# Values of two strided groups as seven half-sized products, behind the third head's projections

## The chip, the cores and the metric

The kernel runs on one core of one Trainium2 chip. The metric is the device time of one execution in microseconds (us). The kernel before takes 1063.59 us (median of 3 runs, 1063.26 to 1063.8).

## The reference

One layer of a hybrid decoder for 512 tokens of width 1024, all in f32. One input projection gives queries, keys and values of three causal token mixers and three gates; the mixers' outputs are gated, added, projected and normed; a squared-ReLU MLP follows. The change is in the values of the third mixer, the dilated attention. Cut to what matters:

```python
DIL_PAIRS = ((128, 1), (512, 4), (2048, 16))   # window, dilation of three head groups, four heads of 128 each
x @ W_in -> da_q da_k da_v (4 heads)  sb_q sb_k sb_v (8 heads)  dl_q dl_k dl_v (3 groups x 4 heads)  gates (3 x 1024)

def dilated_group(q, k, v, bias_table, window, dilation):
    # query t reads keys and values t, t-d, ..., t-window: to_strided puts them in order of t mod d
    logits = einsum(qs, kb) * dh ** -0.5 ; + bias ; causal window
    lse = logsumexp(logits) ; prob = exp(logits - lse)
    o = einsum(prob, vb)
    return o, lse
# the outputs of the three groups of a head slot are combined by softmax over their lse

m = sum_i sigmoid(gate_i) * (branch_i @ W_i)
x = LayerNorm(alpha * x + m @ W_out)
x = LayerNorm(alpha * x + relu(x @ W_up)**2 @ W_down + sigmoid(x @ W_g) * (p @ W_p))
```

The values of the two strided groups (dilation 4 and 16) are two products of x (512 tokens x 1024) with weights of 1024 x 512.

## The kernel before

**Precision.** A product of f32 matrices is made of three matmuls. Each operand is split into a part rounded to the matmul's format and the rest (`wh` and `wl` of a weight, `xh` and `xl` of x), and high x high, high x low and low x high are added up in PSUM. So one output tile of 128 x 512 with a contraction of 1024 takes 8 x 3 = 24 matmuls.

**Weights.** A block of 512 KB (128 x 1024) goes from DRAM into a ring of raw blocks (`raw`, RAW = 7) by a transfer on SP's queue, issued in a fixed order as soon as the block seven places earlier has been used (`fill`). ScalarE casts it to `wh` (L212), VectorE subtracts to `wl` (L214); these two are in a ring of RING = 7 blocks each. `pump` splits blocks ahead up to the ring's size. Other tiles of 128 x 512 (queries, keys, values, forms of x) come from a pool of NSLOT = 42 slots.

**Items.** `main_order` writes out the order of the projection. A "T" item is one tile of queries or keys for 128 columns of weights (L87 to L89, 24 matmuls, one weight block). A "V" item is one tile of values for 128 tokens (L340 to L342, 24 matmuls); four of them share four weight blocks. The loop at the end of `trunk` issues the items one after another and calls `step()` once or twice for each, which advances what stands in `pending`: generators of the attention heads, tables and forms. So the matmuls of a head are put between those of the items, and each engine executes its instructions in the order thus written. A head of the dilated mixer starts when its six T items are done: its logits (L1496 for group 0, L1512 for groups 1 and 2), the bias and the row maxima (VectorE, L1499 and L1520), exponentials (ScalarE, L1505 and L1527), the folding of the maxima and denominators of the three groups (L1530 to L1559), the scaling of the weights (VectorE, L1561 and L1565), their transposes (PE, L1577 and L1586) with evacuations (L96, L98), and the products with the values (L1598, L1603). Only these last ones need the values.

**Strided values.** The values of group 0 are used in the order of the tokens. Those of groups 1 and 2 are needed by residue of the token mod 4: each V item is copied into half a block of the raw ring (a block without a load, `src` None), and four transfers of 64 KB on SP's queue put its rows (`t[c::4]`) into four slots, `by[g][c]`. LAND = 6 steps later they may be used (`by_residue`).

**Order of the values.** In before the three groups' values stand behind the three pairs of T items of the second head (h = 1), one group behind each pair.

**Sums and forms.** Some later products (gates and MLP) are done by Strassen-Winograd's scheme: seven products of half the size instead of eight. It needs sums of weight blocks, which `sum_steps` makes in DRAM ahead of time by copying and accumulating transfers on POOL's queue (L825, L823); the main loop spreads them by a credit of RATES per item, from item 16 on. It also needs sums of parts of x (`mixer_forms`): eight transfers of 256 KB into slots `xr` on POOL's queue, VectorE's differences (L432 to L450), and a split of each of them (cast on ScalarE, L237, and difference on VectorE, L238). The tables of the differential heads are made at item DA_TABS = 41.

Of the kernel before, what the change touches and what calls it, by code (L numbers as in the profile page):

```python
# [10 lines left out]
F32 = mybir.dt.float32  # L11
# [3 lines left out]
OP = mybir.AluOpType  # L15
# [3 lines left out]
P = 128  # L19
# [16 lines left out]
def main_order():  # L36


    o = [("T", "sb_q", 0), ("T", "sb_k", 0), ("T", "sb_q", 1), ("T", "sb_k", 1), ("V", "sb_v", 0)]
    for j in (2, 3):  # L40
        o += [("T", "sb_q", j), ("T", "sb_k", j)]
    for h in range(4):
        for g in range(3):
            o += [("T", "dl_q", 4 * g + h), ("T", "dl_k", 4 * g + h)]
            if h == 1:
                o += [("V", "dl_v", g)]
    for h in range(4):
        o += [("T", "da_q", h), ("T", "da_k", h)]
        if h == 1:
            o += [("V", "da_v", 0)]  # L50
    for j in range(8):
        o += [("T", "gate", 8 + j)]
    return o


def trunk(tc, a, out):
    nc = tc.nc
    es = ExitStack()
    with es:
# [14 lines left out]
        def slot(name, dt=F32):  # L74
            return big.tile([P, 512], dt, name=nm(name), tag="s", bufs=NSLOT)

# [16 lines left out]
        def cp(o, i):  # L93
            flip[0] ^= 1
            if flip[0]:
                nc.scalar.copy(o, i)  # L96
            else:
                nc.vector.tensor_copy(o, i)  # L98
# [220 lines left out]

        by = {}  # L320
        LAND = 6

        def by_residue(g):
            for _ in range(LAND):
                yield
            for c in range(4):
                V["dl_v", g, c] = by[g][c]

        def v_items(nv, name, g):
            blocks = [{"src": None, "w": 1024, "uses": 2, "own": False} for _ in range(2)]  # L330
            if name == "dl_v" and g > 0:
                items[-2]["blocks"] = blocks
            cs = [chunk(a["wv"][nv, c].rearrange("p k n -> p (k n)"), 1024) for c in range(4)]
            for tt in range(4):
                def mm(ps, tt=tt):
                    for k in range(8):
                        c = cs[k // 2]
                        s = slice((k % 2) * 512, (k % 2) * 512 + 512)
                        x1, x2 = xh[k][:, tt * P:tt * P + P], xl[k][:, tt * P:tt * P + P]
                        nc.tensor.matmul(ps, x1, c["h"][:, s], start=k == 0, stop=False)  # L340
                        nc.tensor.matmul(ps, x1, c["l"][:, s], start=False, stop=False)  # L341
                        nc.tensor.matmul(ps, x2, c["h"][:, s], start=False, stop=k == 7)  # L342
                        if k == 3:
                            yield

                def ev(ps, tt=tt):
                    if name == "sb_v":
                        v = [slot(name, F32R).rearrange("p (h two d) -> p h two d", two=2, d=64) for _ in range(2)]
                        pv = ps.rearrange("p (h d) -> p h d", d=64)
                        for i in range(2):  # L350
                            hs = slice(4 * i, 4 * i + 4)
                            nc.scalar.copy(v[i][:, :, 0, :], pv[:, hs, :])
                            nc.vector.tensor_sub(v[i][:, :, 1, :], pv[:, hs, :], v[i][:, :, 0, :].bitcast(F32))
                        V[name, g, tt] = v
                    elif g == 0:
                        t = slot(name)
                        cp(t, ps)
                        V[name, g, tt] = t
                    else:

                        b = blocks[tt // 2]
                        t = b["raw"][:, (tt % 2) * 512:(tt % 2) * 512 + 512]
                        cp(t, ps)
                        if tt == 0:
                            by[g] = [slot(name) for _ in range(4)]
                        for c in range(4):
                            nc.sync.dma_start(by[g][c][32 * tt:32 * tt + 32, :], t[c::4, :])
                        b["uses"] -= 1
                        if tt == 3:
                            pending.append(by_residue(g))  # L370
                item(cs if tt == 3 else [], mm, ev, need=cs)

        nt, nv = 2, 0
# [2 lines left out]
        for kind, name, j in order[2:]:  # L376
            if kind == "T":
                if name == "gate":
                    continue
                t_item(nt, name, j)  # L380
                nt += 1
            else:
                v_items(nv, name, j)
                nv += 1


# [11 lines left out]
                nc.scalar.activation(t, t, AF.Sigmoid, scale=sign)  # L398
            sg[i, j] = t

        HB = slice(0, 256)
        HC = slice(256, 512)
# [4 lines left out]

        def mixer_forms():

            r = {}  # L410
            for h in range(2):
                for th in range(2):
                    for kp in range(2):
                        t = slot("xr")
                        i = nc.gpsimd.dma_start(t.rearrange("p (k t) -> p k t", k=2),
                                                xt[:, 4 * h + 2 * kp:4 * h + 2 * kp + 2, 256 * th:256 * th + 256])
                        tc.add_manual_dep(getattr(i, "ins", i), lows[-1].name, mybir.DependencyInfo(
                            mybir.DependencyClass.Sync, mybir.DependencyReason.DATA), reason="not ahead of time")
                        r[h, th, kp] = t
            r11, r12, r21, r22 = [[r[h, th, kp] for kp in range(2)] for h in range(2) for th in range(2)]  # L420

            def form(p, r):
                fs = [split(r[kp], f"u{p}") for kp in range(2)]
                xf[p] = [[fs[k // 2][i].rearrange("p (k t) -> p k t", k=2)[:, k % 2, :] for i in range(2)]
                         for k in range(4)]
# [7 lines left out]
            form(7, r22)  # L433
# [6 lines left out]
            form(6, r11)  # L440
            yield
            assert not plain_left[0]
            for kp in range(2):
                t = r12[kp].rearrange("p (k t) -> p k t", k=2)
                h, lo = [x[:, 2 * kp:2 * kp + 2, HC] for x in (xhT, xlT)]
                nc.scalar.copy(h, t)
                nc.vector.tensor_sub(lo, t, h.bitcast(F32))
            yield
            for kp in range(2):
                nc.vector.scalar_tensor_tensor(r21[kp], r11[kp], -1.0, r21[kp], op0=OP.mult, op1=OP.subtract)  # L450
            form(4, r21)
            yield

        def branch_item(i, j):
# [339 lines left out]
        dsum = [[dram.tile([P, 1024], F32, name=f"dsum{m}_{i}") for i in range(4)] for m in range(ND - 1)]  # L794

        def sum_steps():
            def up_steps(sums, w):
                w = [w[i].rearrange("p k n -> p (k n)") for i in range(4)]
# [31 lines left out]
            todo = deque(up_steps(gsum[m], a["wg"][m]) for m in range(2))  # L830
# [1015 lines left out]
```

## Time and profile before

| | |
|---|---|
| median of 3 runs | 1063.59 us |
| profiled execution, its own time | 1063.83 us |
| its span | 1062.1 us |
| granted TensorE clock | 0.998 |
| PE (matmul) busy | 1050.6 us |
| DVE (VectorE) busy | 750.0 us |
| ACT (ScalarE) busy | 558.5 us |
| POOL (GpSimd) busy | 130.1 us |
| moved by DMA | 208.21 MB, mean 196 GB/s |

The profile is of one execution. Its span runs from the first instruction to the last; the execution's own time has 1.7 us more around it. In a row of the timeline stand start, duration, engine, line, operation and output <- inputs. In a row of a group stand the line, engine, operation, output <- inputs, shapes, count, then busy time in us and mean duration in ns, then the engine's idle time just before these instructions with what released it. Engines: PE matmul, PEld weight load, DVE VectorE, ACT ScalarE, POOL GpSimd, SP the queue of the weight loads.

### The profile page before, as it was taken

To read this page: it belongs to the slowest core of one execution; us is meant where nothing else is said; L and a number is where in the kernel's file an instruction comes from. 1 tells how busy PE (TensorE), PEld (TensorE's weight loads), DVE (VectorE), ACT (ScalarE), POOL (GpSimd) and SP (SyncE) were. 2 spreads that over 40 slices of the span, in tenths; PEclk is the share of its full clock that TensorE was granted. 3 is DMA by queue.
4 is the path that set the end of the run, shared out by engine and by line. 5 is a ranking of instruction groups with operands and counts; after the bars stand their busy time and mean duration, and the time that the engine had idled before them with its cause. 6 is when DMAs were issued, how large, how long until landed. Compare 5 with 4: busy or idle time off the path is not lost.

```text
span 1062.1 us, 15599 instructions
## 1 busy us (share of the span) xinstructions
PE 1050.6 (99%) x5826; PEld 904.5 (85%) x5826; DVE 750.0 (71%) x1345; ACT 558.5 (53%) x975; POOL 130.1 (12%) x200
## 2 busy tenths in 40 slices
PE   9999999999999999999999999999999999999996
PEld 6888788888888888888999988888999989989885
DVE  6888667548253757768777773888777877877965
ACT  6666545525232546547545452675766665665741
POOL 0000402021121102230111030101110010000000
PEclk9999999999999999999999999999999999999999
DMA  8433656395896819773766583149989688867502
GB/s 314 134 130 99 210 149 168 140 297 135 315 245 193 235 38 316 153 244 98 200 180 202 175 290 137 67 138 268 269 282 276 235 239 255 259 229 244 189 14 79
DMA packets 60987, 208.21 MB, mean 196 GB/s; under 512 B 7944, under 2 KB 8856, under 8 KB 60912
## 3 DMA queue, kind: packets, MB, share of 16 engines
q1 hardware_dynamic: 37728, 125.76, 34.0%
q0 software_dynamic: 22608, 80.55, 29.4%
q8 instruction: 45, 0.74, 0.3%
q10 hardware_dynamic: 576, 0.92, 0.2%
q14 instruction: 30, 0.25, 0.1%
HBM read 202.97 MB, written 73.42 MB: 260 GB/s over the span
## 4 chain that ended last, share of the span: by engine, by line
PE 88%; DVE 7%; issue 2%; ACT 2%; DMA 0%; POOL 0%; SPq 0%; DVEq 0%; POOLq 0%
PE mm L87 13%; PE mm L89 13%; PE mm L88 13%; PE at L87 4%; PE at L983 4%; PE at L984 4%; PE at L985 4%; PE at L88 4%; PE at L89 4%; PE mm L340 3%; PE mm L342 3%; PE mm L341 3%; DVE wl L214 2%; PE at L131 1%; PE at L312 1%
## 5 line engine op out<-in xcount | busy, mean ns | idle before, releaser
L212 ACT CAST wh<-raw 128x1024 fp32r<-128x1024 f32 (+1 forms) x243 | 250.5, 1034 | 253.7 <-PE mm L88 154.5
L214 DVE TENSOR_TENSOR wl<-raw,wh 128x1024 fp32r<-128x1024 f32 (+1 forms) x243 | 291.5, 1205 | 109.8 <-ACT wh L212 106.4
L87 PE MATMUL mm<-xhT,wh 128*128 128x512 f32 x368 | 146.8, 399 | 0.0
L89 PE MATMUL mm<-xhT,wl 128*128 128x512 f32 x368 | 144.4, 392 | 0.0
L88 PE MATMUL mm<-xlT,wh 128*128 128x512 f32 x368 | 144.1, 392 | 0.0
L89 PEld LDWEIGHTS mm<-xhT,wl 128*128 128x128 f32 x368 | 69.1, 188 | 15.0 <-DVE wl L214 0.3
L87 PEld LDWEIGHTS mm<-xhT,wh 128*128 128x128 f32 x368 | 69.2, 188 | 13.6 <-issue 0.4
L88 PEld LDWEIGHTS mm<-xlT,wh 128*128 128x128 f32 x368 | 69.2, 188 | 13.1
L983 PE MATMUL at<-wh,hh 128*128 128x512 f32 x188 | 73.7, 392 | 0.0
L984 PE MATMUL at<-wl,hh 128*128 128x512 f32 x188 | 73.7, 392 | 0.0
L87 PE MATMUL mm<-x1hT,wh 128*128 128x256 f32 x256 | 73.6, 288 | 0.0
L985 PE MATMUL at<-wh,hl 128*128 128x512 f32 x188 | 73.1, 389 | 0.0
L88 PE MATMUL mm<-x1lT,wh 128*128 128x256 f32 x256 | 72.3, 283 | 0.0
L89 PE MATMUL mm<-x1hT,wl 128*128 128x256 f32 x256 | 71.8, 283 | 0.0
L340 PE MATMUL mm<-wh,xhT 128*128 128x512 f32 x160 | 63.4, 396 | 0.0
L342 PE MATMUL mm<-wh,xlT 128*128 128x512 f32 x160 | 62.5, 391 | 0.0
L341 PE MATMUL mm<-wl,xhT 128*128 128x512 f32 x160 | 62.4, 390 | 0.0
L823 POOL DMA_DIRECT2D usum<-in_wu_dram x32 | 28.0, 874 | 232.8 <-DVE wl L214 199.4
L87 PEld LDWEIGHTS mm<-x1hT,wh 128*128 128x128 f32 x256 | 48.8, 190 | 4.7 <-ACT up L917 2.7
L88 PEld LDWEIGHTS mm<-x1lT,wh 128*128 128x128 f32 x256 | 48.8, 191 | 1.5
L89 PEld LDWEIGHTS mm<-x1hT,wl 128*128 128x128 f32 x256 | 48.6, 191 | 0.0
L823 POOL DMA_DIRECT2D dsum<-in_wd_dram x28 | 26.1, 930 | 139.1 <-DVE wl L214 134.8
(437 smaller groups left out, 2538.4 us busy)
## 6 DMA issues: line engine op xcount, KB each, us to landing
usum<-in_wu_dram POOLq DMA_DIRECT2D x48, 512.0 KB, 8.8
raw<-in_wt_dram SPq DMA_DIRECT2D x46, 512.0 KB, 5.7
dsum<-in_wd_dram POOLq DMA_DIRECT2D x42, 512.0 KB, 9.1
raw<-usum SPq DMA_DIRECT2D x32, 512.0 KB, 6.4
raw<-dsum SPq DMA_DIRECT2D x28, 512.0 KB, 4.7
raw<-in_wd_dram SPq DMA_DIRECT2D x25, 512.0 KB, 4.4
raw<-in_wu_dram SPq DMA_DIRECT2D x24, 512.0 KB, 6.1
raw<-in_wv_dram SPq DMA_DIRECT2D x20, 512.0 KB, 5.0
```

The lines of the kernel that those rows point to most:

```text
L87: nc.tensor.matmul(ps, wh, xh, start=start, stop=False, skip_group_check=True)
L88: nc.tensor.matmul(ps, wh, xl, start=False, stop=False, skip_group_check=True)
L89: nc.tensor.matmul(ps, wl, xh, start=False, stop=stop, skip_group_check=True)
L212: i = nc.scalar.copy(h, raw)
L214: i = nc.vector.tensor_sub(lo, raw, h.bitcast(F32))
L340: nc.tensor.matmul(ps, x1, c["h"][:, s], start=k == 0, stop=False)
L341: nc.tensor.matmul(ps, x1, c["l"][:, s], start=False, stop=False)
L342: nc.tensor.matmul(ps, x2, c["h"][:, s], start=False, stop=k == 7)
L823: i = nc.gpsimd.dma_start(o, i, accum_op=OP.add, max_dma_last_dim=4096)
L983: nc.tensor.matmul(ps, h[:, q], c["h"][:, s], start=go, stop=False, skip_group_check=True)
L984: nc.tensor.matmul(ps, h[:, q], c["l"][:, s], start=False, stop=False, skip_group_check=True)
L985: nc.tensor.matmul(ps, lo[:, q], c["h"][:, s], start=False, stop=end, skip_group_check=True)
```

## The change

The values of group 0 stay behind the first pair of T items of the second head. Those of groups 1 and 2 move behind all six T items of the third head and become one block product: x is cut into halves of the tokens and of the contraction, the weights into the two groups and the halves of the contraction, and seven products (p) of half the contraction and half the tokens, in the order 2, 1, 7, 6, 4, 5, 3, take the place of eight. Each is two items (row halves) of 12 matmuls of 128x512, of size 0.5, without a step in their middle: 14 items with 168 matmuls for 8 with 192. They use 14 weight blocks for 8; eight of these (products 7, 6, 5, 3) come from `vsum`, weight sums in DRAM, whose 16 transfers are put first in the queue of sums. `value_forms` loads eight `xr` tiles and makes and splits the sums of x. Evacuations add up the products: 12 operations of VectorE and 6 copies of ScalarE for 8 copies. The results of products 1, 4, 5 and 3 go into raw blocks and from there by 32 transfers of 64 KB, as before. Products 5 and 3 share a PSUM bank each: 3 adds onto 5's sum once that has been read.

Besides, RING goes from 7 to 6 and NSLOT from 42 to 46; the sums start at item 12 at a rate of 1.8 (16 and 1.6 before); DA_TABS goes from 41 to 47; `mixer_forms` shares `load_xr` and `form` with the new forms.

```diff
@@ main_order
-            if h == 1:
+            if h == 1 and g == 0:
                 o += [("V", "dl_v", g)]
+        if h == 2:
+            o += [("V", "dl_v", 1), ("V", "dl_v", 2)]
@@
-        NSLOT = 42
+        NSLOT = 46
-        RING, RAW = 7, 7
+        RING, RAW = 6, 7
@@
+        vf = {p: [(xh[k][:, c], xl[k][:, c]) for k in range(ks, ks + 4)] for p, ks, c in ((1, 0, HB), (2, 4, HB), (3, 4, HC))}
+        vsum = [[dram.tile([P, 1024], F32, name=f"vsum{m}_{i}") for i in range(4)] for m in range(2)]
...
+        def form(to, p, r):
+            fs = [split(r[kp], f"u{p}") for kp in range(2)]
+            to[p] = ...
+        def value_forms():
+            r11, r12, r21, r22 = load_xr()
+            for _ in range(WAIT):
+                yield
+            with tc.issue_after(st["low"]):
+                for kp in range(2):
+                    nc.vector.tensor_sub(r22[kp], r22[kp], r12[kp])
+            form(vf, 7, r22)
+            yield
+            yield
+            for kp in range(2):
+                with tc.issue_after(st["low"]):
+                    nc.vector.tensor_sub(r12[kp], r11[kp], r12[kp])
+                nc.vector.scalar_tensor_tensor(r11[kp], r22[kp], -1.0, r11[kp], op0=OP.mult, op1=OP.subtract)
+            form(vf, 6, r11)
+            yield
+            yield
+            for kp in range(2):
+                nc.vector.scalar_tensor_tensor(r21[kp], r11[kp], -1.0, r21[kp], op0=OP.mult, op1=OP.subtract)
+            form(vf, 4, r21)
+            yield
+            yield
+            form(vf, 5, r12)
+            yield
+        WAIT = 8
+        def value_pair(nv):
+            v_from[:] = len(items) - 5, len(items)
...
+            for p in (2, 1, 7, 6, 4, 5, 3):
+                for r in range(2):
+                    if not r:
+                        blk = {1: 0, 2: 2, 4: 6}.get(p)
+                        cs[p] = [chunk(vsum[kp][{5: 0, 6: 1, 7: 2, 3: 3}[p]] if blk is None else w[blk + kp], 1024)
+                                 for kp in range(2)]
...
+                    def bank(p=p, r=r):
+                        if p == 5:
+                            x[r] = at_bank()
+                        return x[r] if p in (5, 3) else at_bank() if r else mm_bank()
+                    def mm(ps, p=p, r=r):
+                        for k in range(4):
...
+                            nc.tensor.matmul(ps, h[:, q], c["h"][:, n], start=go, stop=False, skip_group_check=True)
+                            nc.tensor.matmul(ps, h[:, q], c["l"][:, n], start=False, stop=False, skip_group_check=True)
+                            nc.tensor.matmul(ps, lo[:, q], c["h"][:, n], start=False, stop=end, skip_group_check=True)
+                    def ev(ps, p=p, r=r):
+                        if p in (2, 7):
+                            s[p, r] = slot("vs")
+                            nc.scalar.copy(s[p, r], ps)
+                        elif p == 1:
+                            s[1, r] = slot("vs")
+                            nc.vector.tensor_add(put(1, r), s.pop((2, r)), ps)
+                            nc.scalar.copy(s[1, r], ps)
+                            send(1, r, 1, 0)
+                        elif p == 6:
+                            nc.vector.tensor_add(s[1, r], s[1, r], ps)
+                            nc.vector.tensor_add(s[7, r], s[7, r], s[1, r])
+                        elif p == 3:
+                            nc.vector.tensor_add(put(3, r), s[1, r], ps)
+                            send(3, r, 1, 1)
+                        else:
+                            nc.vector.scalar_tensor_tensor(put(p, r), s[7, r], -1.0, ps, op0=OP.mult,
+                                                           op1=OP.subtract)
+                            send(p, r, 2, int(p == 5))
+                    item(cs[p] if r else [], mm, ev, need=cs[p], bank=bank, size=0.5)
@@ sum_steps
+            todo = deque(up_steps(vsum[m], [w[2 + i // 2, i % 2 * 2 + m] for i in range(4)], True) for m in range(2))
+            todo.extend(up_steps(gsum[m], a["wg"][m]) for m in range(2))
@@ main loop
-        DA_TABS = 41
+        DA_TABS = 47
-        RATES = 1.6, 1.0
+        RATES = 1.8, 1.0
+            if n == v_from[0]:
+                pending.append(value_forms())
-            if 16 <= n < wout_at - 6:
+            if 12 <= n < wout_at - 6:
```

More of the change, by code (lines that the diff above doesn't have):

```diff
@@ new lines, in load_xr @@
+        def load_xr():
+            r = {}
+            for h in range(2):
+                for th in range(2):
+                    for kp in range(2):
+                        t = slot("xr")
+                        i = nc.gpsimd.dma_start(t.rearrange("p (k t) -> p k t", k=2),
+                                                xt[:, 4 * h + 2 * kp:4 * h + 2 * kp + 2, 256 * th:256 * th + 256])
+                        tc.add_manual_dep(getattr(i, "ins", i), lows[-1].name, mybir.DependencyInfo(
+                            mybir.DependencyClass.Sync, mybir.DependencyReason.DATA), reason="not ahead of time")
+                        r[h, th, kp] = t
+            return [[r[h, th, kp] for kp in range(2)] for h in range(2) for th in range(2)]
@@ new lines, in trunk, with put, send @@
+        WAIT = 8
+        def value_pair(nv):
+            v_from[:] = len(items) - 5, len(items)
+            cs, s, x = {}, {}, {}
+            outs = {p: {"src": None, "w": 1024, "uses": 2, "own": False} for p in (1, 4, 5, 3)}
+            w = [a["wv"][nv + n, c].rearrange("p k n -> p (k n)") for n in range(2) for c in range(4)]
+            def put(p, r):
+                return outs[p]["raw"][:, r * 512:r * 512 + 512]
+            def send(p, r, g, th):
+                tt = 2 * th + r
+                if g not in by:
+                    by[g] = [slot("dl_v") for _ in range(4)]
+                for c in range(4):
+                    nc.sync.dma_start(by[g][c][32 * tt:32 * tt + 32, :], put(p, r)[c::4, :])
+                outs[p]["uses"] -= 1
+            for p in (2, 1, 7, 6, 4, 5, 3):
[4 more added lines that the diff above has]
+                                 for kp in range(2)]
+                        if p in outs:
+                            items[-3]["blocks"] = [outs[p]]
+                    def bank(p=p, r=r):
[3 more added lines that the diff above has]
+                    def mm(ps, p=p, r=r):
+                        q = slice(r * P, r * P + P)
+                        for k in range(4):
+                            c = cs[p][k // 2]
+                            n = slice(k % 2 * 512, k % 2 * 512 + 512)
+                            h, lo = vf[p][k]
+                            go, end = k == 0 and p != 3, k == 3 and p != 5
+                            nc.tensor.matmul(ps, h[:, q], c["h"][:, n], start=go, stop=False, skip_group_check=True)
[20 more added lines that the diff above has]
+                            send(p, r, 2, int(p == 5))
+                        if (p, r) == (3, 1):
+                            pending.append(by_residue())
+                    item(cs[p] if r else [], mm, ev, need=cs[p], bank=bank, size=0.5)
@@ L358, in ev @@
                         V[name, g, tt] = t
[L359 to L370, printed above, removed]
                 item(cs if tt == 3 else [], mm, ev, need=cs)
@@ L382, in trunk @@
             else:
-                v_items(nv, name, j)
+                if name != "dl_v" or j == 0:
+                    v_items(nv, name, j)
+                elif j == 1:
+                    value_pair(nv)
                 nv += 1
@@ L408, in mixer_forms @@
         def mixer_forms():
[L410 to L425, printed above, removed]
+            r11, r12, r21, r22 = load_xr()
             for _ in range(8):
@@ L796, in sum_steps, with up_steps @@
         def sum_steps():
-            def up_steps(sums, w):
-                w = [w[i].rearrange("p k n -> p (k n)") for i in range(4)]
+            def up_steps(sums, w, flat=False):
+                w = [w[i] if flat else w[i].rearrange("p k n -> p (k n)") for i in range(4)]
                 a1, a2, a3, a4 = sums
@@ L828, in issue @@
                     mybir.DependencyClass.Sync, mybir.DependencyReason.DATA), reason="spread over the main stream")
-            todo = deque(up_steps(gsum[m], a["wg"][m]) for m in range(2))
+            w = a["wv"].rearrange("g c p k n -> g c p (k n)")
+            todo = deque(up_steps(vsum[m], [w[2 + i // 2, i % 2 * 2 + m] for i in range(4)], True) for m in range(2))
+            todo.extend(up_steps(gsum[m], a["wg"][m]) for m in range(2))
             for m in range(ND):
```

26 lines of the change are left out of this document (14 added, 12 removed).

## The prediction

> **What bounds the kernel now.** I read the page first (busy shares, slices, chain), then PE's waits, then PE's timeline for the price of a matmul, then windows of 20 us around the place to which the work moves, then VectorE by group and in order.
>
> ```profile
> PE 1050.6 (99%) x5826; PEld 904.5 (85%) x5826; DVE 750.0 (71%) x1345; ACT 558.5 (53%) x975; POOL 130.1 (12%) x200
> PE 88%; DVE 7%; issue 2%; ACT 2%; DMA 0%; POOL 0%; SPq 0%; DVEq 0%; POOLq 0%
> PE at L1153 <- DVE zero L1150: 1.3, 1, 1.3
> PE at L1444 <- DVE lg L1439: 0.6, 2, 0.4
> ```
>
> TensorE is busy for 1050.6 of 1062.1 us, the chain that ended last is 88% PE, and of the waits that the view names for PE the longest is 1.3 us, at the start. So a matmul taken away is time taken away, as long as nothing else makes PE wait. VectorE is second, with 71% on average; an average hides stretches, so it is read by stretch below. The profiled execution took 1063.83 us, 1.7 us more than its span and 0.24 us above the median of 1063.59. I make the sum against 1063.83 and take 0.24 off at the end. About 0.2%, 2.1 us, is what a measurement of this kernel tells from no change: below 1061.5 is faster, above 1065.7 slower.
>
> **1. The matmuls removed.** The two strided groups' values are 8 items of 24 matmuls of 128x512, 192 in all. Seven products of two row halves with 12 matmuls each are 168. 24 go. A duration would price them wrongly:
>
> ```profile
> 84.46 0.39 PE L87 MATMUL mm<-xhT,wh 128*128 128x512 f32 x1
> 84.69 0.39 PE L88 MATMUL mm<-xlT,wh 128*128 128x512 f32 x1
> ...
> 89.90 0.39 PE L87 MATMUL mm<-xhT,wh 128*128 128x512 f32 x1
> ```
>
> Each lasts 0.39 us, but from 84.46 to 89.90 there are 24 starts, so one costs 5.44 / 24 = 0.2267 us. 24 of them are **5.4 us**, not the 9.4 that 24 x 0.39 would give. This term has no cover: it is on the path.
>
> **2. VectorE in the stretch that receives the values.** The values now stand behind the third head's six projections, and the first two dilated heads' softmaxes, which need the values only at their end, run beside them. In before the same two heads and the third group's values fall here:
>
> ```profile
> 240.00:260.00 20.00, 20.00 (x119) 17.51 (x118) 15.49 (x83) 13.34 (x41) 2.19 (x3) 1.00 0.34 99
> 260.00:280.00 20.00, 20.00 (x98) 16.77 (x97) 9.85 (x21) 5.36 (x8) 4.44 (x8) 1.00 1.03 362
> 280.00:300.00 20.00, 20.00 (x110) 17.36 (x109) 3.83 (x4) 4.65 (x6) 4.67 (x7) 1.00 0.80 225
> L214 DVE TENSOR_TENSOR wl<-raw,wh 128x1024 fp32r<-128x1024 f32 x9 | 11.0, 1221 | 8.8 <-ACT wh L212 8.8
> L291 DVE COPY dl_k<-mm 128x512 f32<-128x512 f32 x3 | 2.1, 692 | 17.2 <-PE mm L89 17.2
> L98 DVE COPY raw<-mm 128x512 f32<-128x512 f32 x2 | 1.4, 688 | 6.9 <-PE mm L342 6.9
> ```
>
> The window rows give, after the range, its length and then busy time of PE, PEld, DVE, ACT and POOL, granted clock, DMA share, GB/s; the three lower rows are VectorE's groups from 238 to 300 us. VectorE is busy for 15.49 + 9.85 + 3.83 = 29.2 us of 60. Less 11.0 of weight splits, 2.1 and 1.4 of copies, two heads are 14.7 us by durations. A head has some 35 small operations, and those start later than they last:
>
> ```profile
> 261.95 0.20 DVE L1558 RECIPROCAL mxx<-mxx 128x8 f32<-128x8 f32 x1
> 262.19 0.17 DVE L1559 TENSOR_TENSOR mxx<-mxx,ex 128x8 f32<-128x8 f32 x1
> 262.39 1.08 DVE L1561 TENSOR_SCALAR L<-L,mxx 128x128 f32<-128x128 f32 x4
> ```
>
> 0.24 us from start to start against 0.20. With 70 x 0.04 = 2.8 more, two heads take about 17.6 us. The large operations go the other way. The gate products of before, which use the same kind of forms, show it:
>
> ```profile
> 480.00:500.00 20.00, 20.00 (x117) 17.57 (x116) 18.82 (x32) 15.84 (x29) 1.53 (x3) 1.00 0.25 82
> 491.05 0.69 DVE L447 TENSOR_TENSOR xlT<-xr,xhT 128x512 fp32r<-128x512 f32 x1
> 491.78 0.69 DVE L238 TENSOR_TENSOR u6l<-xr,u6h 128x512 fp32r<-128x512 f32 x1
> 492.39 0.68 DVE L447 TENSOR_TENSOR xlT<-xr,xhT 128x512 fp32r<-128x512 f32 x1
> 492.99 0.69 DVE L238 TENSOR_TENSOR u6l<-xr,u6h 128x512 fp32r<-128x512 f32 x1
> 493.60 0.68 DVE L468 TENSOR_TENSOR graw<-graw,mm 128x512 f32<-128x512 f32 x1
> 494.19 0.69 DVE L450 SCALAR_TENSOR_TENSOR xr<-xr,xr 128x512 f32<-128x512 f32 x1
> 494.80 1.22 DVE L214 TENSOR_TENSOR wl<-raw,wh 128x1024 fp32r<-128x1024 f32 x1
> 495.93 0.42 DVE L523 TENSOR_TENSOR graw<-at,up 128x256 f32<-128x256 f32 x1
> ```
>
> An operation of 0.69 us is followed after 0.60 (491.78, 492.39, 492.99, 493.60, 494.19), a weight split of 1.22 after 1.13 (494.80, 495.93). In the built order of the changed program these stand on VectorE between the first head's first logits and the last evacuation of the seven products: 16 weight splits (14 of the products, two of neighbours), 14 form operations, 12 evacuations and the two heads: 16 x 1.13 + 26 x 0.60 + 17.6 = **51.3 us**. PE's work there: 14 half items, 168 x 0.2267 = 38.1, one projection 5.4 (24 matmuls), and the two heads' logits and transposes:
>
> ```profile
> L1512 PE MATMUL at<-dl_k,dl_q 128*128 128x128 f32 x32 | 4.0, 277 | 0.0
> L1496 PE MATMUL at<-dl_k,dl_q 128*128 128x256 f32 x12 | 2.9, 380 | 0.0
> L1586 PE MATMUL at<-ident,L 128*128 128x128 f32 x16 | 2.1, 272 | 0.0
> L1577 PE MATMUL at<-ident,L 128*128 128x128 f32 x14 | 2.0, 272 | 0.0
> ```
>
> 11.0 us in these groups of PE between 238 and 270 us, which overlap like the matmuls above; I take 8. Together **51.5 us**. The two engines are equal. That has two consequences. VectorE's waits inside the heads are no longer free:
>
> ```profile
> L1530 DVE TENSOR_TENSOR r<-st,exf 128x32 f32<-128x32 f32 x2 | 0.4, 188 | 2.0 <-ACT L L1505 2.0
> L1533 DVE TENSOR_TENSOR r<-st,exf 128x32 f32<-128x32 f32 x2 | 0.4, 192 | 1.0 <-ACT L L1527 0.9
> L1543 DVE TENSOR_TENSOR sel<-at,pick 128x64 f32<-128x64 f32 x2 | 0.4, 221 | 0.9 <-PE at L1539 0.9
> ```
>
> 3.9 us in these three groups, for two heads. Unfilled, they make 51.3 + 3.9 - 51.5 = 3.7 us by which VectorE ends behind PE. And the lateness is felt, because PE works in a fixed order: the transposes L1577 and L1586 of the first head need its scaled logits (L1561, L1565) and stand ahead of the sixth and seventh products' matmuls, so all matmuls behind them wait. Walking both engines' built orders with these prices, I get a wait of some 2.7 us before the first head's transposes, 1.4 before the second's, and none after, 4.1 together. Bounds: 0 if splits of the ring run ahead and fill the heads' gaps; and with full durations for the large operations (16 x 1.22 + 26 x 0.69 + 17.6 = 55.1 us) 55.1 + 3.9 - 51.5 = 7.5. I take **3.5**, a little under the walk, since the form operations stand between a head's steps and fill part of its gaps.
>
> By the Trainium skill, VectorE: DVE Perf Modes, section Terms, entry DRAIN, the pipe is flushed after every operation and the next one can't issue until it is empty. By that rule durations would add up in full, and the sum for the stretch would be the 7.5 just named. The rows above (0.60 between starts, 0.69 long) speak against it for large operations and for it only with the small ones.
>
> **3. ScalarE.** 6 more weight casts, 8 form casts and 2 more copies net (6 against 4):
>
> ```profile
> L212 ACT CAST wh<-raw 128x1024 fp32r<-128x1024 f32 (+1 forms) x243 | 250.5, 1034 | 253.7 <-PE mm L88 154.5
> L96 ACT COPY pt<-at 128x512 f32<-128x512 f32 x3 | 1.7, 586 | 0.0
> ```
>
> 6 x 1.03 + 10 x 0.59 = 12.1 us on top of the 13.34 + 5.36 + 4.65 = 23.4 us of these 60: 35.5 of 51.5. Nothing, with 16 us to spare; if a head's exponentials queue behind two casts, 2 us, once.
>
> **4. Transfers.** Six more weight blocks of 512 KB, eight x blocks of 256 KB, and 16 more weight sums in DRAM on POOL's queue. The 32 transfers of 64 KB remain, later.
>
> ```profile
> DMA  9999999999814301202999999999999994019999
> GB/s 236 240 262 295 420 418 422 367 215 239 217 48 121 141 0 55 80 0 20 307 231 279 227 372 417 424 422 416 420 416 422 422 256 82 0 43 291 207 211 315
> raw<-in_wv_dram SPq DMA_DIRECT2D x3, 512.0 KB, 5.3
> gsum<-in_wg_dram POOLq DMA_DIRECT2D x2, 512.0 KB, 8.5
> ```
>
> These rows are of 220 to 300 us: up to 424 GB/s are moved when much is queued, and there are idle slices; 249 GB/s is the mean (19.95 MB in 80 us). The 5 MB of blocks add 5 / 57 us = 88 GB/s: about 340. One block per 2.7 us is wanted for 38 us against 5.3 us of landing, and 7 raw plus 6 split blocks stand ahead: if blocks came only one each 5.3 us, 38 / 5.3 = 7 would come, 14 are used, and the 7 missing come out of 13 ahead. The sums are the first in their queue and at 8.5 us each overlap. They begin at item 12 instead of 16, at 1.8 per item instead of 1.6, so that 16 more of them fit: those of the fifth to eighth block are wanted first by the third product. I take 0; a late sum would hold SP's queue with the blocks behind it, up to one landing, 8.5 us, less the cover.
>
> **5. Ring of 6.** PE frees a block, then cast and split follow.
>
> ```profile
> L214 DVE TENSOR_TENSOR wl<-raw,wh 128x1024 fp32r<-128x1024 f32 x235 | 286.2, 1222 | 109.7 <-ACT wh L212 106.4 <-PE at L1458 2.0
> ```
>
> With 1.03 + 1.22 and a hand-over that is 2.3 to 2.4 us. In PE's times of before, the first use of a block comes at least 5.7 us after the last use of the block six earlier, everywhere in the gates, the MLP and the tail. 3.3 us are left, so I take 0. If ScalarE and VectorE come 3 us late at the tightest places (about eight of them), 0.2 to 1 us each: up to 5.
>
> **6. Rates, tables.** The differential tables come at item 47 instead of 41, behind as many half items more, so at the same place of the stream; 0 to 0.5 us either way. Four more slots of 2 KB a partition pay for the ring's block; no wait shows for them.
>
> **Sum.** 1063.83 - 5.4 + 3.5 = 1061.9, less 0.24: **1061.6 us**. With the second term at its bounds: 1058.2 to 1065.7.
>
> **The rivals.**
> *Full gain.* VectorE keeps up: the window at 480 us is 18.82 of 20 us busy while PE stays at 20.00, so 94% doesn't hold PE where no chain through the heads runs. Against it: 51.3 of 51.5 us and heads that were built for slack. 1063.6 - 5.4 = 1058.2.
> *VectorE decides the stretch (slower).* The order of the two heads and of the third and fourth behind them (now closer together) puts splits, forms and evacuations into the heads' chain of logits, exponentials and transposes; when PE waits, its evacuations come later too, and these hold the banks. From a VectorE total of 57 us on, against PE's 51.5, the change loses. At 55.1 + 3.9 = 59 in this stretch and 2 us in the next heads: stall 7.5 + 2 = 9.5, 1067.7; with single waits up to 14 us, 1072. For it: durations, and a fixed order. Against: the measured starts.
> By the Trainium skill, TensorE: Matmul & The Clock Gate, Part 1, a gap of more than about 3.4 us halves the clock for as long; that would add an estimated 1.7 us to each such wait. The clock column above shows 1.00 in each window, and no gap of that length has been there to test it.
> *The ring of 6 starves PE.* Up to 5 us spread over MLP and tail: 1061.6 + 4 = 1065.6 or so, and 1069 at most. Against it: 3.3 us to spare.
> *The change doesn't do what it says*: sums or x blocks land late, SP's queue stands still behind the third product's weights, PE waits 4 to 8 us: 1065 to 1069.
>
> **How the numbers follow.** Forecast (stall 1.5 to 6.5) 0.42, around 1061.6, about half of it below 1061.5; full gain 0.21; VectorE decides 0.24; ring 0.06; late transfers 0.07. Faster: 0.21 + 0.21 = 0.42. Within 0.2%: 0.20 of the forecast, and 0.09 of the last three, 0.29. Slower: 0.29. The range leaves out the dearest tenth above and a tenth below full gain's centre: 1057.8 to 1069.0. The likeliest case's own range is 1059.7 to 1064.7.
>
> **What would show it.** PE has 24 matmuls of 128x512 fewer. In the stretch of the seven products VectorE is busy for over 90% and PE's waits name L (the scaled logits) at the transposes of the first and second head, 2.7 and 1.4 us. No PE wait names wl or wh in the MLP; the lead of a split over its use falls there but stays above 3 us. The x blocks land before the first form operation. I am wrong if PE waits less than 1 us there (full gain), if one wait at a transpose or an evacuation is over 5 us, if the MLP's length changes by over 1 us, or if PE waits for a load.

## The result and the profile after

The changed kernel takes 1077.38 us (median of 4 runs, 1076.08 to 1078.53) against 1063.69 us of before in the same comparison: a ratio of 1.0128 (95% interval 1.0111 to 1.0146). It is 13.7 us slower. The forecast was 1061.6 and the range ended at 1069.0, so the prediction was wrong, in sign too. The profiled execution took 1077.6 us, with a span of 1075.9.

The page of the changed kernel: engine totals, the chain that ended last, and the slices of PE and of its granted clock.

```profile
PE 1049.2 (98%) x5802; PEld 902.3 (84%) x5802; DVE 771.2 (72%) x1375; ACT 569.0 (53%) x991; POOL 147.7 (14%) x224
PE   9999999999959999999999999999999999999996
PEclk9999999999989999999999999999999999999998
PE 83%; DVE 7%; DMA 4%; ACT 2%; issue 2%; POOL 0%; SPq 0%; DVEq 0%; ACTq 0%; POOLq 0%
```

The 24 matmuls are gone (5802 for 5826). In the twelfth slice PE falls to half, and the granted clock falls with it. The chain has a new member, DMA with 4%. PE's waits name it:

```profile
PE at L1697 <- DMA dl_v<-raw: 11.1, 1, 11.1
PE at L1671 <- DVE L L1655: 1.9, 3, 1.3
PE at L1247 <- DVE zero L1244: 1.3, 1, 1.3
```

(L1697, L1692, L1671 are the lines L1603, L1598, L1577 of before.) One wait of 11.1 us, for one of the last eight of the 64 KB transfers that put the strided values in order. The windows of the stretch (columns as before: length, busy time of PE, PEld, DVE, ACT, POOL, clock, DMA share, GB/s) show what else is there:

```profile
240.00:260.00 20.00, 18.71 (x107) 15.98 (x106) 19.11 (x88) 13.94 (x43) 1.65 (x2) 1.00 0.51 125
260.00:280.00 20.00, 19.60 (x98) 16.01 (x97) 18.75 (x37) 12.61 (x18) 4.73 (x7) 1.00 0.74 187
280.00:300.00 20.00, 20.00 (x89) 16.17 (x88) 7.55 (x8) 5.76 (x6) 5.37 (x9) 1.00 1.04 340
300.00:320.00 20.00, 9.84 (x44) 8.06 (x44) 4.73 (x6) 2.60 (x3) 4.55 (x7) 0.84 1.06 304
320.00:340.00 20.00, 19.09 (x92) 16.79 (x93) 5.03 (x16) 4.63 (x12) 2.55 (x4) 0.82 0.92 285
```

From 240 to 280 us VectorE is the busy engine, 19.11 and 18.75 of 20 us, as forecast, and PE loses 1.7 us. Then VectorE is idle most of the time (7.55 and 4.73 of 20 us busy) and the transfer engines are full, with a share of 1.04 and 1.06. The transfers from 280 to 325 us:

```profile
DMA  9999999999999999999999999999999999999999
raw<-in_wt_dram SPq DMA_DIRECT2D x6, 512.0 KB, 11.4
usum<-in_wu_dram POOLq DMA_DIRECT2D x3, 512.0 KB, 12.8
dl_v<-raw SPq DMA_DIRECT2D x20, 64.0 KB, 9.7
```

There is not one idle slice in 45 us. A transfer of 64 KB takes 9.7 us from issue to landing (median of 20; 9.2 over all 32). In before the same transfers landed after 2.9 us (median of all 32). VectorE's and SP's timelines and the chain show how the last one gets late:

```profile
299.35 1.22 DVE L216 TENSOR_TENSOR wl<-raw,wh 128x1024 fp32r<-128x1024 f32 x1 [4.73 <-ACT wh L214]
300.49 1.28 DVE L441 TENSOR_TENSOR raw<-vs,at 128x512 f32<-128x512 f32 x2
302.66 1.10 SPq L400 DMA_DIRECT2D dl_v<-raw  x2
309.88 0.47 SPq L400 DMA_DIRECT2D dl_v<-raw  x1
315.72 0.47 SPq L400 DMA_DIRECT2D dl_v<-raw  x1
309.88 10.94 DMA dl_v<-raw
```

PE ends the third product at 292.1 us. Its evacuation (L441) stands on VectorE behind a weight split that waits for its block, so it comes at 300.5, 8.4 us late. The eight transfers are then issued between 302.66 and 315.72, because SP's queue works in order, has weight blocks between them, and each transfer waits for the landing of the one that used its semaphore (the counter by which a landing is signalled) before, eight places ahead: the one of 309.88 goes out when the one of 300.83, eight issues earlier, has landed (309.82). It lands at 320.82 and ends PE's wait. The heads' products with the strided values stand in PE's order three items behind the last product and are reached at 309.84, before the last four transfers are issued. In before there was room: the last of these transfers was issued at 260.41, and PE came to the first product that needs it at 280.36, 20 us later.

Behind the gap the clock is low. Windows of 2 us, and PE's timeline of the two heads' products in the changed kernel, then in before:

```profile
322.00:324.00 2.00, 2.00 (x9) 1.86 (x9) 0.00 (x0) 0.00 (x0) 0.53 (x1) 0.50 1.07 416
326.00:328.00 2.00, 2.00 (x10) 1.71 (x10) 0.00 (x0) 0.00 (x0) 0.00 (x0) 0.68 1.08 279
328.00:330.00 2.00, 2.00 (x17) 1.92 (x17) 0.00 (x0) 0.42 (x1) 0.00 (x0) 1.00 1.07 281
```

```profile
320.91 4.18 PE L1697 MATMUL at<-pt,dl_v 128*128 128x128 f32 x16 [11.07 <-DMA dl_v<-raw]
324.88 2.87 PE L1692 MATMUL at<-pt,dl_v 128*128 128x256 f32 x8
327.59 1.95 PE L1697 MATMUL at<-pt,dl_v 128*128 128x128 f32 x16
```

```profile
280.36 1.95 PE L1603 MATMUL at<-pt,dl_v 128*128 128x128 f32 x16
282.15 1.68 PE L1598 MATMUL at<-pt,dl_v 128*128 128x256 f32 x8
283.67 1.95 PE L1603 MATMUL at<-pt,dl_v 128*128 128x128 f32 x16
```

The same 24 matmuls take 327.59 - 320.91 = 6.7 us instead of 283.67 - 280.36 = 3.3: 3.4 us lost at a granted clock of 0.50. By the Trainium skill, TensorE: Matmul & The Clock Gate, Part 1, an idle gap of over about 3.4 us halves the clock until PE has been busy again for at least about as long. The trace agrees in kind (gap 11.1 us, clock 0.50, then 1.00 by 328); but PE worked at 0.50 for about 6 us, and the estimate from that page in the prediction, 1.7 us, was half of what was lost. A gap of 2.13 us was followed by a low clock too (first experiment, 0.54), so here 3.4 us is not the least gap that counts.

The sum for PE: -5.4 (matmuls) + 11.1 (wait) + 3.4 (clock) + 1.9 (L1671) = 11.0. Measured, the start of PE's last matmul is at 1065.31 instead of 1053.76, 11.55 us later, so half a microsecond is not placed. The remaining 2.2 us of the span lie behind the last matmul: 10.6 us to the end of the span, 8.3 before.

### The profile page after: what moved, and what is told of

Same layout as the page of the kernel before. It is cut to its first block, busy times and chain, and to the rows that moved or that the text cites. A ratio compares the mean times of both kernels' runs of the same rounds, so it can differ in the third digit from the quotient of the medians.

```text
span 1075.9 us, 15638 instructions
## 1 busy us (share of the span) xinstructions
PE 1049.2 (98%) x5802; PEld 902.3 (84%) x5802; DVE 771.2 (72%) x1375; ACT 569.0 (53%) x991; POOL 147.7 (14%) x224
## 4 chain that ended last, share of the span: by engine, by line
PE 83%; DVE 7%; DMA 4%; ACT 2%; issue 2%; POOL 0%; SPq 0%; DVEq 0%; ACTq 0%; POOLq 0%
PE mm L89 13%; PE mm L90 12%; PE mm L91 12%; PE at L89 4%; PE at L1077 4%; PE at L1078 4%; PE at L1079 4%; PE at L91 4%; PE at L90 4%; DMA dl_v<-raw 3%; DVE wl L216 2%; PE mm L459 2%; PE mm L461 2%; PE mm L460 2%; PE at L133 1%
## 5 line engine op out<-in xcount | busy, mean ns | idle before, releaser
L214 ACT CAST wh<-raw 128x1024 fp32r<-128x1024 f32 x249 | 256.9, 1035 | 265.0 <-PE mm L90 149.4
L216 DVE TENSOR_TENSOR wl<-raw,wh 128x1024 fp32r<-128x1024 f32 x249 | 298.6, 1205 | 115.3 <-ACT wh L214 112.2
L91 PEld LDWEIGHTS mm<-xhT,wl 128*128 128x128 f32 x368 | 69.1, 188 | 14.7
L1079 PEld LDWEIGHTS at<-wh,hl 128*128 128x128 f32 x188 | 35.3, 188 | 7.7
L1077 PEld LDWEIGHTS at<-wh,hh 128*128 128x128 f32 x188 | 35.5, 189 | 6.0
L1078 PEld LDWEIGHTS at<-wl,hh 128*128 128x128 f32 x188 | 35.5, 189 | 5.5
```

The lines of the kernel that those rows point to most:

```text
L91: nc.tensor.matmul(ps, wl, xh, start=False, stop=stop, skip_group_check=True)
L214: i = nc.scalar.copy(h, raw)
L216: i = nc.vector.tensor_sub(lo, raw, h.bitcast(F32))
L1077: nc.tensor.matmul(ps, h[:, q], c["h"][:, s], start=go, stop=False, skip_group_check=True)
L1078: nc.tensor.matmul(ps, h[:, q], c["l"][:, s], start=False, stop=False, skip_group_check=True)
L1079: nc.tensor.matmul(ps, lo[:, q], c["h"][:, s], start=False, stop=end, skip_group_check=True)
```

## The experiments

Three theories stood at the start. *Full engines*: sums, weight blocks and 64 KB transfers together fill the transfer engines, and everything lands late. *Queue*: SP's order makes the transfers late. *VectorE*: the prediction's own. Each run is given with its median, its ratio to before measured beside it, and the 95% interval of that ratio.

**No sums beside the products.**

```diff
-            if 12 <= n < wout_at - 6:
-                credit += it["size"] * (RATES[0] if n < pairs_at[0] else RATES[1])
+            if v_from[1] - 2 <= n < v_from[1] + 22:
+                pass
+            elif 12 <= n < wout_at - 6:
+                credit += it["size"] * (RATES[0] if n < pairs_at[0] else RATES[1]) * (1.6 if n > v_from[1] else 1.0)
```

> The changed kernel, with no weight sums on POOL's queue from two items before the seven products to the eighth item behind them; the sums left out are caught up by 1.6 times the rate afterwards. Full-engines theory (the sixteen DMA engines are at a share of 1.03 to 1.06 from 280 us on, so that each 64 KB transfer of the values lands after 9.7 us): the landing falls to 3 to 5 us, the wait of PE at L1697 (11.1 us) is gone, the clock stays at 1.00, and the time is 1060 to 1063 us. Queue theory (SP's queue issues the 32 transfers in order behind weight blocks, each waiting for the transfer eight places ahead): the issue of the last one still comes 10 us or more behind its evacuation, PE waits 5 us or more, 1068 to 1074 us. VectorE theory of the prediction: no change, 1077.

1074.03 us, ratio 1.010 (1.0084 to 1.0115). The total missed the expectation of the full-engines theory and lies at the upper end of the queue theory's, but the signs are those of full engines. Its waits, the 64 KB transfers from 280 to 310 us, POOL's timeline, and the clock and PE's timeline at the first of two new waits:

```profile
PE at L1570 <- DVE on L1564: 8.6, 2, 6.5
DVE on L1564 <- POOL ms L1562: 15.6, 2, 11.7
dl_v<-raw SPq DMA_DIRECT2D x19, 64.0 KB, 3.4
507.39 0.52 POOL L917 DMA_DIRECT2D dsum<-dsum  x1 [11.24 <-DVE wl L216]
507.93 1.04 POOL L1562 TENSOR_TENSOR ms<-ms,mhalf 128x4 f32<-128x4 f32 x1
441.15 0.66 PE L1570 MATMUL at<-ident,on 128*128 128x128 f32 x4 [2.13 <-DVE on L1564]
442.00:444.00 2.00, 2.00 (x8) 1.61 (x7) 1.97 (x3) 0.79 (x3) 1.04 (x2) 0.54 1.01 369
```

The transfers land after 3.4 us, the evacuation comes at 296.2 instead of 300.5, the last issue at 301.8 instead of 315.7, and there is no wait for `dl_v`, though SP's order is unchanged. PE reaches the first differential head 4.7 us ahead of before (3.8 from 371 us on, where both kernels' matmuls again stand in the same order). That gain is lost later: the sums caught up beside the differential heads put those heads' small operation (L1562) in POOL's order behind a step that waits for a weight split, and PE waits 8.6 us for its result. With a low clock behind both gaps, PE's stream falls from 3.8 us ahead to 8.7 behind. These were new waits made by the experiment.

The pause also lets the four 256 KB transfers `sh<-rv` of the differential tables go earlier: they stand on POOL's queue behind the sums, go out at 280.4 to 290.0 us in the changed kernel and at 272.6 to 277.8 here. No run takes away the sums alone. But in the changed kernel these four have landed by 303.2 us, and six of the last eight 64 KB transfers are issued after that and still take 6.8 to 10.9 us.

**The transfers on ScalarE's queue.** `nc.sync.dma_start` becomes `nc.scalar.dma_start` in `send`.

> The changed kernel with the 32 transfers of 64 KB issued on ScalarE's queue instead of SP's. Queue theory: issue follows the evacuation within 2 us (14 us before), the last lands some 10 us behind the evacuation at 301 us, so PE's wait falls from 11.1 to 0 to 3 us: 1061 to 1066 us. Full-engines theory alone: landing stays near 10 us and the wait at 8 us or more: 1072 us or more. If ScalarE's exponentials are held by the issues, PE waits at the transposes instead: 2 to 4 us more.

1077.38 us, ratio 1.0131 (1.0116 to 1.0146): no gain, and neither expectation was met: the landing came down to 7.3 us and the wait at L1697 to 5.6.

```profile
PE at L1697 <- issue: 2.9, 1, 2.9
PE at L1697 <- DMA dl_v<-raw: 2.7, 3, 1.2
ACT wh L214 <- DMA dl_v<-raw: 30.0, 3, 14.1
dl_v<-raw ACTq DMA_DIRECT2D x22, 64.0 KB, 7.3
```

The queue's wait moves to ScalarE, which holds its weight casts for 30.0 us behind the issues. What PE no longer waits for at L1697 it loses elsewhere (2.6 us for `dl_q`, 1.8 for `vs`, and the low clock). The in-order wait moved along with the transfers, so this run alone does not separate the two theories. The first run does: with SP's order as it was and the engines not full (a share of 0.67 from 280 to 300 us and 0.51 from 300 to 320), the lateness was gone. The order of the queue passes lateness on. The Trainium skill, Trainium Kernel Development and Optimization, section Key Constraints, says that transfers issued from the three queues share the same 16 engines and that several issuing engines only save issue time; this run agrees (share 1.05, landing 7.3 us).

**The products with the values later.** `LAND = 14` instead of 6.

> The changed kernel with LAND = 14 instead of 6: the products with the strided values stand eight steps, about 20 us of PE, later in PE's order. Both theories of a late landing: the wait of 11.1 us and the slow clock behind it are hidden, 1060 to 1064 us. If the landing only moves along (SP's queue blocked by blocks that the later items free), the wait stays over 5 us: 1070 us or more. VectorE theory: 1077.

1064.16 us, ratio 1.0008 (0.9999 to 1.0017), just above the time expected. The wait and the slow clock are gone with landings as slow as ever (10.2 us median from 280 to 325 us): what costs is the lateness against PE's order, not the slowness itself. PE's last matmul is 1.66 us ahead of before, not some 5; the rest of the gain goes into small waits (2.1 us at L1671, 1.1 at L1552, 1.0 for `dl_q`) and into the 10.6 us behind the last matmul.

**Plain values at the new place.** The two groups' values as eight items of 24 matmuls behind the third head, DA_TABS back at 41.

> The changed kernel with the values of the two strided groups as eight plain items of 24 matmuls at the new place behind the third head's projections; its 16 sums in DRAM are still made but not read. Place theory (the later place alone makes the transfers late): PE waits 8 us or more for dl_v, 1075 to 1083 us. Products theory (14 blocks and the evacuations of seven products in 38 us make them late): the wait is below 3 us, and the time is that of before with up to 3 us more, 1063 to 1068 us.

1065.3 us, ratio 1.0014 (1.0005 to 1.0024). No wait for `dl_v`: the last issue is at 297.6, the landing 5.5 us (median of 32). The place costs little by itself, but it takes part of the room: from the last issue to the first product that needs the values (313.17) there are 15.6 us, for landings of up to 12.7. In before there were 20 us, for landings of up to 9.5. The engines are as full here (1.04 from 280 to 320 us) and PE does not wait, so full engines alone are not enough either: with the seven products the last issue comes 18 us later, at 315.7. Whether their blocks, their spacing or their evacuations do that was not tested apart.

**RING 6 alone.** The kernel before with RING 6 and NSLOT 46.

> The kernel before with RING 6 and NSLOT 46, nothing else. The shift of PE's stream in the changed kernel is flat from the first product of the MLP to the end (11.54 to 11.55 us), so the ring theory is expected to fall: 1063.4, within 1 us. Ring theory: 1 to 5 us slower. The time from PE's last matmul to the end of the span stays at 8.3 us.

1063.05 us, ratio 0.9996 (0.9987 to 1.0005). The smaller ring costs nothing.

**Caught up later.** The first pause, without the factor 1.6, and `RATES = 1.8, 2.4`, so that the sums are caught up beside the gate products.

> The changed kernel with the pause of the sums around the seven products as before (no sums from two items before them to the eighth behind them), but caught up only from the gate products on (2.4 per item instead of 1.0), not beside the differential heads. Theory (the pause takes away the wait for dl_v; the 8.6 us at L1570 of the first pause came from the differential heads' small operation on POOL, queued behind caught-up sums): no wait for dl_v and none over 1 us at L1570; PE's stream at the first differential head 4.7 us ahead of before and so to its end; with the 2.3 us that the changed kernel has more behind its last matmul, 1061 us, and 1059 if those go. Rival (a pause only moves the crowding, to the gate products): PE waits there for weights or POOL, 1063 to 1070.

1059.41 us, ratio 0.9961 (0.9948 to 0.9973): faster than before. PE's stream is 4.8 us ahead at the first differential head (3.9 from 371 us on) and 4.0 at the end, and 7.7 us lie behind the last matmul.

**A shorter pause and LAND = 9.**

```diff
+            if v_from[1] + 4 <= n < v_from[1] + 20:
+                pass
-        LAND = 6
+        LAND = 9
-        RATES = 1.8, 1.0
+        RATES = 1.8, 1.8
```

> The changed kernel with a shorter pause (from the fifth half item of the products to the 20th item behind their start), LAND = 9, and the sums caught up at 1.8 per item in the gate products. If the landing is a matter of degree, half a pause and half the delay suffice: no wait for dl_v, 1060 to 1062 us. If the pause is too short, PE waits 1 to 4 us for dl_v: 1063 to 1066.

1057.4 us, ratio 0.9944 (0.993 to 0.9958). At this rate one sum of the MLP's weights is read 5.4 us before its last step is issued, so a part of that sum is left out; the time stands for the same number of instructions. The same at a rate of 2.1, with whole sums:

> The changed kernel with the short pause (fifth half item of the products to the 20th item behind their start), LAND = 9, and the sums caught up at 2.1 per item in the gate products. Theory (late transfers alone cost the gain; the seven products' VectorE load costs 0.7 us net): no wait for dl_v, PE's stream 4.7 to 5.8 us ahead of before from the differential heads on, 1057 to 1059 us. Rival (the prediction's own VectorE term of 3.5 us is real and only hidden): 1061.6.

1057.13 us, ratio 0.994 (0.9928 to 0.9953), the fastest of all: 6.5 us faster than before (1063.61 beside it).

```profile
PE at L1671 <- DVE L L1655: 1.7, 2, 1.3
240.00:260.00 20.00, 18.71 (x108) 15.96 (x107) 19.03 (x88) 14.28 (x43) 0.00 (x0) 1.00 0.23 74
260.00:280.00 20.00, 19.59 (x98) 16.00 (x97) 18.84 (x34) 12.27 (x18) 2.20 (x4) 1.00 0.61 198
300.00:320.00 20.00, 20.00 (x100) 17.02 (x99) 7.32 (x10) 5.26 (x7) 4.24 (x5) 1.00 0.99 284
```

VectorE is as full as in the changed kernel (19.03 and 18.84), and PE loses 1.7 us to it (1.29 + 0.41 in these two windows). PE stays at 20.00 where it stood still.

**Half the sums.** The rate halved over the window of the first pause, `RATES = 1.8, 1.8`.

> The changed kernel with half the rate of sums (0.9 per item) over the window in which the first pause had none, caught up at 1.8 in the gate products. A matter of load: the 64 KB transfers land after 4 to 7 us (9.7 at the full rate, 3.4 without sums), the wait for dl_v is 0 to 4 us, 1060 to 1066 us. If the sums matter only by their number in flight, not by the load: wait near 11 us, 1075 us.

1070.81 us, ratio 1.0065 (1.0051 to 1.0079), above the time expected.

```profile
PE at L1697 <- DMA dl_v<-raw: 5.5, 2, 5.1
dl_v<-raw SPq DMA_DIRECT2D x18, 64.0 KB, 9.9
300.00:320.00 20.00, 14.50 (x63) 12.31 (x62) 3.14 (x3) 3.07 (x4) 1.63 (x2) 0.85 1.03 288
```

The wait goes by the amount of sums: 11.1 us at the full rate, 5.5 at half, 0 without. The landing between 280 and 310 us does not: 9.9 us at half the rate (the four transfers `sh<-rv` of the differential tables are there too), 3.4 without. As I read it, load decides how long the engines are full, and so how many of the 32 transfers are caught: at half the rate the share is down to 0.38 from 320 to 340 us, at the full rate it is 0.92.

**Control.** The kernel before with a pause over items 36 to 46, LAND = 9 and `RATES = 1.6, 1.7`.

> Control: the kernel before with the same kind of pause over the same time (items 36 to 46), LAND = 9, and the sums caught up at 1.7 in the gate products. If the gain of the mended kernels is that of the seven products: no change, 1063.4 within 1 us. If the pause itself pays: 1060 us or less.

1063.49 us, ratio 1.0003 (0.9994 to 1.0012). The pause gives nothing to before, which has no wait for `dl_v` to lose. So the gain of the mended kernels is that of the change. The plain values at the new place with the pause were not run. That the products and not the place make the gain rests on the size: 24 matmuls are 5.4 us, and PE's last matmul is 5.75 us ahead in the fastest kernel.

**What lies behind the last matmul.** 48 small transfers more on POOL's queue in the kernel before.

> The kernel before with 48 small extra transfers of 32 KB on POOL's queue (DRAM to DRAM, not read) at items 60 to 107. From PE's last matmul to the end of the span before takes 8.3 us, the changed kernel, with 24 more transfers on POOL's queue, 10.6, and the one with 16 more 9.5. Count theory (the end of the program takes about 0.09 us for each transfer of that queue): 12.6 us here, the time 1068 us. If the bytes or something else of the changed kernel make it: 8.3 us and 1063.5.

1063.06 us, ratio 0.9997 (0.9988 to 1.0006), and 7.8 us behind the last matmul. The count theory falls. Over the profiles this stretch was 7.7 to 8.4 us (before, the control, RING 6, the three pauses that are caught up beside the gate products, this run), 9.5 (plain values) or 10.5 to 10.6 (the changed kernel, the first pause, ScalarE's queue, LAND 14, half the sums). The last output transfers are issued and landed alike in all of them (2.0 to 2.3 us); the difference lies behind it, where the profile shows no instruction. Its cause stays open.

## Why the prediction was wrong, step by step

**The matmuls (step 1): right.** 24 fewer, and with the late transfers removed PE's last matmul is 5.75 us ahead (1048.01 against 1053.76 in the fastest kernel).

**VectorE (step 2): right in kind, too dear.** VectorE was to be busy over 90% of the stretch, with waits named L at the heads' transposes: it is busy 95% from 240 to 280 us, and the wait is there. It is 1.9 us in three pieces, not 4.1 in two. The term was 3.5. Across the whole stretch the late pause loses 2.6 of the 5.4 us (its stream is 1.1 us ahead at 238 us and 3.9 from 371 us on), and the fastest kernel 1.3 (from 1.0 to 5.1, at 391 us); not all of that need be VectorE's. The walk probably let too much of the heads' idle time stay unfilled; no run tests that. The 7.5 of full durations is refuted: PE lost 1.7 us from 240 to 280 us.

**ScalarE and ring (steps 3, 5): right.** PE's longest wait for ScalarE is 0.5 us, and 0.6 in before. The shift of PE's stream is 11.5 us from the last product of the mixer to the last matmul, and RING 6 alone is 0.9996.

**Transfers (step 4): the step that failed.** "I take 0" should have been 11.1 + 3.4 = 14.5 us. Three things were wrong in it. It asked whether the weight blocks come in time, which have 13 blocks of cover, and not whether the 32 transfers of 64 KB do, which it named only as "remain, later"; their cover is LAND, three items or some 16 us. It judged room by GB/s (340 wanted, up to 424 seen). The amount was right, 340 GB/s from 280 to 300 us, but it came with a share of 1.04: the engines were full. A row quoted in it already had a share of 1.03 at 362 GB/s, and other rows of before show the same:

```profile
220.00:240.00 20.00, 20.00 (x95) 16.77 (x94) 7.31 (x16) 3.65 (x6) 3.24 (x5) 1.00 1.05 311
raw<-in_wt_dram SPq DMA_DIRECT2D x9, 512.0 KB, 8.4
dl_v<-raw SPq DMA_DIRECT2D x16, 64.0 KB, 4.9
```

The engines were full in such windows of before too, below the best rate. The two lower rows stand in the same view of 220 to 300 us from which the prediction took the 5.3 us of a weight block: other blocks needed 8.4 us, and the 64 KB transfers 4.9. And it took a mean over 80 us, where the sums, the tables' transfers and the blocks behind the products meet from 280 us on. What stood nearest was the rival of late transfers with 0.07, but for sums and x blocks and at 4 to 8 us; no wait of PE names the x blocks or the sums.

**Rates, tables (step 6): not settled.** They were priced at 0 to 0.5 us. Without sums beside the products and with a late catch-up the same kernel keeps its gain, so the sums that run there matter; what the step from 1.6 to 1.8 per item adds, and what the tables add, no run shows.

**Two slips of the working, without weight.** 14.7 + 2.8 us for the two heads are 17.5, not 17.6, and the sum is 1061.7 rather than 1061.6.

**The slower rival (VectorE) did not decide.** The slower side came from a transfer on which it had no eye. The low clock that it named did come, behind another wait.

## To carry over

When work moves later, list what each of its results must still pass (evacuation, queue, landing) before it is used, and hold that against the distance in PE's order; transfers that stay the same in number may have lost their cover. Judge room on the transfer engines by their busy share in the very stretch, not by GB/s and not by a mean, and take background transfers out of a stretch in which a short transfer is awaited. A background stream that is caught up later must not share an in-order queue with a small operation on the path.

## Not expected of the hardware

One wait of 11.1 us cost 14.5: the clock was 0.50 for about 6 us behind it. Over 20 us, the transfer engines show a share of 1.03 to 1.06 at anything from 286 to 362 GB/s when accumulating transfers are among them; a 64 KB transfer that lands in 3.4 us beside weight blocks alone then needs 9.7.
